# Sums of squares, token sums and weight sums in other places of a hybrid encoder block

## The chip, the cores and the metric

The kernel runs on one core of one Trainium2 chip. The core has TensorE (matmuls, results in PSUM banks), DVE (VectorE), ACT (ScalarE) and POOL (GpSimd), and DMA transfers that here are all issued from the queue of SP (SyncE). Each engine carries out its own instructions in order. The metric is the time of one execution on the device, in microseconds (us).

## The reference, cut to what matters

One layer over 2048 tokens of width 1024, all in float32. The change lies in the first steps: the input norm, the combined projection, and what each of the two head groups makes of its columns.

```python
xn = rms_norm(h, ln_mix_g[l])               # x / sqrt(mean(x*x) + EPS) * gain
proj = xn @ w_in[l]                         # 2048 x 1024 by 1024 x 2512
y_a = mlstm_group(q, k, v, o, gates, ...)   # columns of proj; q, k: conv over tokens, silu
y_b = mla_group(c_q, c_kv, k_rope, ...)     # latent queries and keys: norm, w_uq, w_ukv, rope, softmax
h = h + concatenate([y_a, y_b]) @ w_out[l]
h = h + conv_gated_mlp(rms_norm(h, ln_ffn_g[l]), ...)
h = h + sigmoid(rms_norm(h, ple_norm_g[l]) @ w_ple_gate[l]) * rms_norm(p[l] @ w_ple_proj[l], ple_post_g[l])
return rms_norm(h, final_g)
```

## The kernel before, in words

Every float32 operand of a large product is split in two parts of a shorter type, `hi` (a cast on ACT) and `lo` (a subtraction on DVE); a product takes three matmuls (`mm3`, `prod`). The instruction order on each engine is made by a planner that follows the program's order but moves an instruction ahead when its operands are ready in the planner's model; inside `manual_schedule` the named engine keeps the program's order. Buffers are named places (`w0`, `x11`, `u2`, `t7`): taking a place again waits until its last readers are done.

**Input projection** (`in_proj`). 16 tiles of 128 tokens. For each tile x is loaded turned (`load_x`), split (`split_x`) and multiplied with 464 columns of gates and latents (`nat` with `wr`, then `rest`), and with 512 value columns (`vals`). The norm's factor of a tile, `rcol`, is made by `ssq_x` and `rms_x`: ACT squares the turned tile (L236), DVE adds the eight blocks to two (L238, L239), TensorE sums over partitions with a matrix of ones (L244), DVE scales (L248) and POOL takes the power (L249). `rest` scales the latents with it, norms and rotates them into `nn`, and `turn_rest` turns `nn` by four transposes on TensorE (L290) and stores it as `rest_d`. `norm_row` turns the factors of eight tiles into a row in memory, `r_d`.

Beside the tiles a generator, `work`, is advanced by a step after each group of matmuls: first `weight_sums`, which for six pairs of weight tiles makes the sums S1 to S4 and stores them (`sp_d`), then from the ninth tile `token_sums`, which makes the seven token operands of the first block of 1024 tokens (B11, T1, T2, B21, T3, T4, B22), and last `pair_begin`, which loads and splits the first pair's operands.

**Pairs** (`pairs`). A product of two by two blocks is done with seven block products (a Winograd form), 12 matmuls each, for 6 pairs of weight tiles and 2 blocks of tokens: 12 rounds, `i` = 0 to 11. `pair_load(i)` fetches weights and their stored sums two rounds ahead, `pair_prep(i)` splits them a round ahead. The generator `sums` in `pairs` makes the second block's token operands in the rounds 1 to 4, and `load` splits them in the rounds 5 and 6. Results are added on DVE (L511), go through the convolution (`conv`) or, for the output gate, a sigmoid, and are stored (L577) as `qk_d` and `o_d`. For the output gate the store reads the buffer of the sums (places `u0` to `u2`) in place. `gates` makes the forget and input gates of all chunks in the rounds 6 to 10, one step at each `side`.

**Latent queries** (`queries`). For each of 8 groups of 256 tokens: `rope` (TensorE, then 12 small DVE instructions, L836 to L838), `weights` (first four groups: values' weights times output weights), `turn` of the rotated queries, and `latent` in two halves. PSUM results come from `gbank`, which goes round four banks. Score banks (`bank`, four others) are used only by the input projection and the scores. `attend_begin` scores the first tile of queries after the seventh group.

**mLSTM and attention** run side by side after that; in the mLSTM the heads' outputs are scaled (L1163) by factors that POOL makes (`rsq`, L145).

## Time and profile before

| | us |
|---|---|
| median of 3 runs | 2889.65 |
| lowest and highest of the 3 | 2887.4 and 2890.66 |
| the profiled execution, whole | 2890.04 |
| its span, first to last instruction | 2887.9 |
| ACT busy in the span | 1577.4 |
| DVE busy in the span | 2138.3 |

The granted clock of TensorE over the span is 0.997 of full. The profile lists instructions by source line (L545 is line 545), engine and operands (`out<-in`). A line of a helper stands for all who call it: L122 and L125 are the two halves of every split, L135 every matmul of `mm3`. Idle time before an instruction is put down to what released it ("<-DVE uv L511"). The order of time gives for each piece its start, its length from the first start to the last end, and how many instructions were merged; ends of matmuls are modelled and reach into the next one.

### The profile page before, as it was taken

How to read it: one execution, taken by the hardware profiler on the slowest of the kernel's cores; microseconds unless marked ns; L12 is line 12 of the kernel's file. 1: busy time of each engine (PE TensorE's matmuls, PEld its weight loads, DVE VectorE, ACT ScalarE, POOL GpSimd, SP SyncE). 2: the span in 40 equal slices, each digit the busy share in tenths (PEclk: the TensorE clock that was granted, in tenths of full speed). 3: DMA queues.
4: the chain of work that ended last, by engine and by line, in shares of the span. 5: the costliest groups of instructions: out<-in, count | busy, mean ns of one | idle time of the engine just before them, and what ended most of it. 6: DMA issues, size and time to landing. Idle time of an engine off the chain costs nothing.

```text
span 2887.9 us, 40258 instructions
## 1 busy us (share of the span) xinstructions
PE 2822.1 (98%) x13970; PEld 2364.1 (82%) x13970; DVE 2138.3 (74%) x3751; ACT 1577.4 (55%) x3037; POOL 213.0 (7%) x331
## 2 busy tenths in 40 slices
...
GB/s 250 239 218 285 248 186 233 173 164 145 126 136 115 97 106 111 114 239 290 276 142 167 198 167 148 221 182 237 232 229 211 239 185 252 162 267 209 280 201 164
DMA packets 455139, 566.36 MB, mean 196 GB/s; under 512 B 35316, under 2 KB 303640, under 8 KB 454936
## 3 DMA queue, kind: packets, MB, share of 16 engines
...
q8 instruction: 110, 1.80, 0.3%
q14 instruction: 93, 0.76, 0.1%
...
## 4 chain that ended last, share of the span: by engine, by line
PE 77%; DMA 8%; DVE 6%; ACT 4%; issue 3%; POOL 1%; SPq 1%; POOLq 0%; ACTq 0%; DVEq 0%
PE fy L1736 21%; PE fz L1736 14%; PE fx L1736 14%; PE ppv L1275 3%; PE tb L1263 3%; PE bk L135 2%; PE bk L1203 2%; PE bk L1200 2%; PE bk L1204 2%; PE bk L1201 2%; PE bk L1202 2%; PE ppv L1276 2%; PE fs L135 1%; PE fy L545 1%; DMA fwr<-in_w_in 1%
## 5 line engine op out<-in xcount | busy, mean ns | idle before, releaser
L1736 PE MATMUL fz<-op,fw 128*128 128x512 f32 x1968 | 478.8, 392 | 4.2 <-ACT fw L122 4.2
L1736 PE MATMUL fx<-op,fw 128*128 128x512 f32 x1968 | 476.6, 390 | 2.1 <-ACT fy L1849 1.2
L1736 PE MATMUL fy<-op,fw 128*128 128x512 f32 x1968 | 475.0, 390 | 0.0
L1736 PEld LDWEIGHTS fz<-op,fw 128*128 128x128 f32 x1968 | 368.4, 188 | 81.7 <-ACT fw L122 5.0
L1736 PEld LDWEIGHTS fx<-op,fw 128*128 128x128 f32 x1968 | 368.0, 188 | 79.2 <-ACT fy L1849 1.6
L1736 PEld LDWEIGHTS fy<-op,fw 128*128 128x128 f32 x1968 | 368.6, 188 | 76.5 <-DVE fh L1721 0.2
L122 ACT CAST pt<-tb 128x512 fp32r<-128x512 f32 x256 | 147.0, 586 | 198.9 <-PE tb L1263 198.0
L1736 PE MATMUL fy<-op,fwd 128*128 128x512 f32 (+1 forms) x984 | 238.5, 390 | 0.5 <-DVE p L1721 0.3
L1205 DVE TENSOR_REDUCE mx<-bk 128x1 f32<-128x512 f32 x256 | 174.9, 685 | 65.5 <-PE bk L1204 63.1
L1736 PEld LDWEIGHTS fy<-op,fwd 128*128 128x128 f32 x984 | 182.5, 188 | 38.9 <-DVE p L1721 0.8
L125 DVE TENSOR_TENSOR pt<-tb,pt 128x512 fp32r<-128x512 f32 x256 | 173.3, 685 | 34.4 <-ACT pt L122 33.0
L1275 PE MATMUL ppv<-pt,kv 128*128 128x512 f32 x512 | 187.9, 406 | 1.0 <-DVE pt L125 1.0
L1222 ACT ACTIVATE pe<-bk,nm 128x512 f32<-128x512 f32 x256 | 174.5, 698 | 17.8 <-DVE nm L1216 16.4
L125 DVE TENSOR_TENSOR op<-opr,op 128x512 fp32r<-128x512 f32 x205 | 134.0, 690 | 34.2 <-ACT op L122 34.2
L122 ACT CAST op<-opr 128x512 fp32r<-128x512 f32 x205 | 119.8, 620 | 71.4 <-DMA opr<-tw_d 16.5
L1263 PE MATMUL tb<-ident,pe 128*128 128x128 f32 x1024 | 150.7, 273 | 3.4 <-DVE pt L125 3.2
L1276 PE MATMUL ppv<-pt,kv 128*128 128x256 f32 x512 | 144.0, 281 | 0.0
L1263 PEld LDWEIGHTS tb<-ident,pe 128*128 128x128 f32 x1024 | 122.3, 140 | 23.6 <-DVE pt L125 6.0
L125 DVE TENSOR_TENSOR fw<-fwr,fw 128x1024 fp32r<-128x1024 f32 x100 | 122.0, 1220 | 24.3 <-ACT fw L122 24.3
L122 ACT CAST fw<-hraw 128x1024 fp32r<-128x1024 f32 (+1 forms) x72 | 70.2, 980 | 115.7 <-PE fx L1736 58.9
L1784 DVE SCALAR_TENSOR_TENSOR fgv<-uv,fcw,fgv 128x1024 f32<-128x1024 f32 x88 | 112.8, 1282 | 16.9 <-ACT fgv L1782 16.2
L122 ACT CAST fw<-fwr 128x1024 fp32r<-128x1024 f32 x100 | 105.0, 1051 | 36.4 <-DVE fwr L1710 21.6
...
## 6 DMA issues: line engine op xcount, KB each, us to landing
fwr<-in_w_up SPq DMA_DIRECT2D x66, 512.0 KB, 4.9
fh<-h_d SPq DMA_DIRECT2D x48, 512.0 KB, 4.5
h_d<-fh SPq DMA_DIRECT2D x48, 512.0 KB, 4.1
s_d<-fwr SPq DMA_DIRECT2D x44, 512.0 KB, 2.7
fws<-s_d SPq DMA_DIRECT2D x44, 512.0 KB, 4.2
rw<-row_d SPq DMA_DIRECT2D x32, 512.0 KB, 5.4
...
```

The costliest lines, as they stand in the source:

```text
L122: nc.scalar.copy(hi, src)
L125: (sub or nc.vector).tensor_tensor(lo, src, _f(hi), op=ALU.subtract)
L135: mm = lambda *a, **k: self.nc.tensor.matmul(*a, **k, skip_group_check=more)
L1200: mm(ps, ql, kh[:, ks], start=True, stop=False)
L1201: mm(ps, qr, self.krl[:, ks], start=False, stop=False)
L1205: nc.vector.tensor_reduce(s.mx[:, kb:kb + 1], ps, axis=AX.X, op=ALU.max)
L1222: nc.scalar.activation(s.pe[:, kb % 2], s.banks[kb], AF.Exp, bias=s.nm, accum_out=s.rs[:, kb:kb + 1])
L1263: nc.tensor.transpose(t[:, j, :], s.p[kb][:, j * P:(j + 1) * P], self.ident)
L1275: mm(w.ps, vh[:, ks], pts[kb][:, j], start=kt == 0, stop=False, skip_group_check=True)
L1276: mm(w.ps[:, 0], vl[:, ks], pts[kb][:, j, 0], start=False, stop=kt == NT - 1, skip_group_check=True)
L1736: nc.tensor.matmul(out, a[:, k * P:(k + 1) * P], parts[lo][:, cols], start=first, stop=lo == 1 and k == last, skip_group_check=more)
L1784: nc.vector.scalar_tensor_tensor(t, u[:, tap:tap + 2 * SB], self.taps[:, tap, ct:ct + 1], t, op0=ALU.mult, op1=ALU.add)
```

## The change

The sums of squares are taken from a second load of x, by rows: `square` loads 128 tokens by 1024 and lets one ACT instruction square and add them up; POOL scales and takes the power. All 16 are issued by the fifth tile. The factors' rows follow at the fifth and seventh tile, and `token_sums` makes both blocks' operands in the input projection, from the sixth tile on (the second block's are stored). `weight_sums` and `sp_d` are gone: `pair_load` fetches both weight tiles whole and `pair_prep` makes the four sums for each pair, in both blocks. `turn_rest` runs a tile later. At the start ACT has one small instruction ahead of the data, x is fetched ahead of the weights, and TensorE runs 26 transposes ahead of the first product. In the pairs, `gates` moves from the rounds 6 to 10 to 1 to 4, every second `side`; the output gate is stored from the places `w7` and `w11`; two edge copies move from DVE to ACT; the last round's two remaining products change places. In the latent queries the first six groups' `rope` and second half of `latent`, and all of `weights`, use score banks; the splits of keys and values are spread over groups; the first scores come a group earlier. In the mLSTM one of four pauses moves ahead of L1163.

```diff
-        self.sp_d = dt([6, 2, P, D], F32, name="sp_d")
...
-        def ssq_x(st):
-            sq = self.at("u2", [P, KT, P], name="x_sq")
-            nc.scalar.activation(sq, xq[st], AF.Square)
-            t = ss[st] = self.at("t7", [P, 4, P], name="x_ss")
-            nc.vector.tensor_tensor(t, sq[:, 0:4], sq[:, 4:8], op=ALU.add)
-            nc.vector.tensor_tensor(t[:, 0:2], t[:, 0:2], t[:, 2:4], op=ALU.add)
-
-        def rms_x(st):
-            ps = self.pml.tile([P, 4], F32, name="ssp", tag="ml")
-            for i in range(2):
-                m = nc.tensor.matmul(ps, ss[st][:, i], ones, start=i == 0, stop=i == 1)
-                if i == 0:
-                    self.tc.keep_in_program_order(m)
-            t = self.stat(1, "rsm")
-            nc.vector.tensor_scalar(t, ps[:, 0:1], 1.0 / D, EPS, op0=ALU.mult, op1=ALU.add)
-            nc.gpsimd.tensor_tensor(rcol[:, st:st + 1], t, self.nhalf[:, :1], op=ALU.pow)
-
-        def nat(st, ws, n):
+        rows = _rot("", ("u2", "x10", "x11"))
+
+        def square(st):
+            t = self.at(next(rows), [P, D], name="x_row")
+            nc.sync.dma_start(t, d["x"][0, st * P:(st + 1) * P, :])
+            sq = self.stat(1, "nt_s")
+            nc.scalar.activation(t, t, AF.Square, accum_out=sq)
+            self.rsq(sq, 1, 1.0 / D, rcol[:, st:st + 1])
+
+        def nat(st, ws, n, warm=0):
             ps = self.bank()
+            for _ in range(warm):
+                nc.tensor.transpose(ps[:, :P], self.ident, self.ident)
...
+        nc.scalar.activation(self.stat(1, "warm"), self.nhalf[:, 0:1], AF.Copy, scale=2.0)
         load_x(0)
         raws = []
         for f in range(2):
-            raws.append(load_raw(OFF_R, NREST, f, 2))
...
             nc.sync.dma_start(xq[0][:, fs], d["x_turned"][:, fs, 0:P])
             split_x(0, fs)
+            raws.append(load_raw(OFF_R, NREST, f, 2))
         raws += [load_raw(OFF_R, NREST, k2) for k2 in (2, 3)]
         wr = split_w(raws, NREST, rest_place)
         load_x(1)
+        square(0)
+        split_x(1)
...
-        ssq_x(0)
-        split_x(1)
         raws = [load_raw(OFF_V, 512, k2) for k2 in range(4)]
-        ps = nat(0, wr, NREST)
-        rms_x(0)
-        rest(0, ps)
-        ssq_x(1)
+        square(1)
+        rest(0, nat(0, wr, NREST, 26))
         wv = split_w(raws, 512, val_place)
         load_x(2)
-        ps = nat(1, wr, NREST)
-        rms_x(1)
-        rest(1, ps)
+        rest(1, nat(1, wr, NREST))
...
+        work = chain(self.token_sums(), self.pair_begin())
...
+            if st in (4, 6):
+                norm_row(st // 2 - 2)
...
+            rest(st, nat(st, wr, NREST))
+            if st < 5:
+                for q in range(4 * st - 4, 4 * st):
+                    square(q)
+            else:
+                next(work, None)
+            turn_rest(st - 1)
...
-    def weight_sums(self):
-
-        nc = self.nc
...
-            tt(v[:, hi], v[:, lo], v[:, hi], op=ALU.add)
-            tt(v[:, lo], g[:, lo], v[:, lo], op=ALU.subtract)
-            nc.sync.dma_start(self.sp_d[pr, 0], v)
-            yield
...
+            if i < 7:
+                nxt = load(i + 1)
...
+            store(blk, "B22", k, b[:, H])
+            if blk:
+                store(blk, "B11", k, a[:, L])
+                store(blk, "B21", k, b[:, L])
+                yield
+                tt(a[:, H], a[:, H], a[:, L], op=ALU.subtract)
+                store(blk, "T1", k, a[:, H])
+                c = self.at("u2", [P, 2, SB], name="xsc")
+                tt(c[:, 0], b[:, H], a[:, H], op=ALU.subtract)
+                store(blk, "T2", k, c[:, 0])
+                yield
+                tt(c[:, 1], c[:, 0], a[:, L], op=ALU.subtract)
+                store(blk, "T3", k, c[:, 1])
+                t4 = self.at("t7", [P, SB], name="xsd")
+                tt(t4, b[:, L], c[:, 0], op=ALU.subtract)
+                store(blk, "T4", k, t4)
+                yield
+                continue
...
     def pair_load(self, i):
 
-        nc, pr = self.nc, i % 6
-        g = self.at("w12", [P, KT, P], name="fwr")
-        nc.sync.dma_start(g, self.w_tile(pr, 0))
-        v = self.at("w13", [P, 4, P], name="fwr")
-        nc.sync.dma_start(v, self.w_tile(pr, 1, 4))
-        sv, sg = [self.at(t, [P, D], name="fws") for t in ("w0", "w1")]
-        nc.sync.dma_start(sv, self.sp_d[pr, 0])
-        nc.sync.dma_start(sg, self.sp_d[pr, 1])
-        self.raw[i] = g, v, sv, sg
+        raw = []
+        for e in range(2):
+            t = self.at(("w12", "w13", "w0", "w1")[i % 2 * 2 + e], [P, KT, P], name="fwr")
+            self.nc.sync.dma_start(t, self.w_tile(i % 6, e))
+            raw.append(t.rearrange("p k c -> p (k c)"))
+        self.raw[i] = raw
 
     def pair_prep(self, i):
 
-        flat = lambda t: t.rearrange("p k c -> p (k c)")
-        g, v, sv, sg = self.raw.pop(i)
+        tt = self.nc.vector.tensor_tensor
+        lo, hi = slice(0, SB), slice(SB, 2 * SB)
+        g, v = self.raw.pop(i)
         ops = self.ops[i] = {}
-        ops["A11"], ops["A12"] = self.up_pair(flat(g))
+        ops["A11"], ops["A12"] = self.up_pair(g)
+        d = self.at(("w10", "w2")[i % 2] if i else "u0", [P, 2, SB], F32R, "fwd")
+        self.split(v[:, hi], d[:, 0], d[:, 1])
+        ops["A22"] = d[:, 0], d[:, 1]
         yield
-        ops["S3"], ops["S1"] = self.up_pair(sv)
+        tt(v[:, hi], v[:, lo], v[:, hi], op=ALU.add)
+        tt(v[:, lo], g[:, lo], v[:, lo], op=ALU.subtract)
+        ops["S3"], ops["S1"] = self.up_pair(v)
         yield
-        ops["S2"], ops["S4"] = self.up_pair(sg)
+        tt(g[:, lo], v[:, hi], g[:, lo], op=ALU.subtract)
+        tt(g[:, hi], g[:, hi], g[:, lo], op=ALU.subtract)
+        ops["S2"], ops["S4"] = self.up_pair(g)
         yield
-        d = self.at(("w10", "w2")[i % 2], [P, 2, SB], F32R, "fwd")
-        self.split(flat(v), d[:, 0], d[:, 1])
-        ops["A22"] = d[:, 0], d[:, 1]
 
     def pair_begin(self):
 
         self.npair = 1
         self.pair_load(0)
+        self.pair_load(1)
         yield
         yield
-        self.begun = self.pair_prep(0)
-        for _ in range(3):
-            next(self.begun)
-            yield
+        yield from self.pair_prep(0)
...
-                t = u[:, 1:1 + 2 * SB]
-                nc.scalar.activation(t, t, AF.Copy, scale=go[:, h:h + 1])
+                t = self.at(("w7", "w11")[half], [P, 2 * SB], name="ct")
+                nc.scalar.activation(t, u[:, 1:1 + 2 * SB], AF.Copy, scale=go[:, h:h + 1])
...
-                    nc.vector.tensor_copy(edge[:, ch:ch + 1], u[:, 2 * SB:2 * SB + 1])
-                    nc.vector.tensor_copy(part[:, ch:ch + 1], t[:, 2 * SB - 1:2 * SB])
+                    nc.scalar.copy(edge[:, ch:ch + 1], u[:, 2 * SB:2 * SB + 1])
+                    nc.scalar.copy(part[:, ch:ch + 1], t[:, 2 * SB - 1:2 * SB])
...
-        def sums():
...
-                for i in (1, 3, 0, 2):
-                    nc.sync.dma_start(t[i], d["x_turned"][:, k + i // 2 * 4, (2 + i % 2) * SB:(3 + i % 2) * SB])
...
+        gates, prev = self.gates(), None
...
-                if gates:
+                if 0 < i < 5 and at % 2:
                     self.gate_bank = prev.spare if at % 2 else s.spare
                     next(gates, None)
...
+        rest_z(prev)
         rest_y(prev)
-        rest_z(prev)
...
-        w = [self.at(t, [P, D], F32R, "woa") for t in (("w7", "w11"), ("w3", "w4"))[h % 2]]
+        t = self.at(("x3", "x7")[h % 2], [P, 2, D], F32R, "woa")
+        w = t[:, 0], t[:, 1]
...
-                ps = self.gbank()
+                ps = self.bank()
...
-            ps = self.gbank([P, 2, NH, 64], "qpr")
+            ps = (self.bank if c < 6 else self.gbank)([P, 2, NH, 64], "qpr")
...
-            ps = self.gbank([P, 2, 256])
+            ps = (self.bank if half and c < 6 else self.gbank)([P, 2, 256])
...
-                if c == 1:
-                    self.vh, self.vl = self.split_latent(2, ("x10", "x11"))
-                if c == 2:
-                    self.kr2, self.krl = self.split_latent(1, ("x14", "x15"))
+                if c in (1, 3):
+                    kr = self.split_latent(1, ("x14", "x15"), (c - 1, c), None if c == 1 else kr)
+                if c in (4, 5, 6, 7):
+                    vv = self.split_latent(2, ("x10", "x11"), (c - 4,), None if c == 4 else vv)
...
+                    self.kr2, self.krl = kr
                     att = self.attend_begin()
                     next(att)
-                if c == 6:
-                    next(att)
-            next(att)
+                if c > 4:
+                    next(att, None)
...
             r4 = self.rsq(ssq, NH, 1.0 / P)
+            yield
             nc.vector.tensor_tensor(hh, hh, r4.unsqueeze(2).broadcast_to([P, NH, P]), op=ALU.mult)
-            yield from pause(4)
+            yield from pause(3)
```

129 lines of the change are left out of this document (31 added, 98 removed).

## The prediction

> **What bounds the kernel now.** I read the head of the page first, for the share of each engine, then the busy time by stage, then who waited for whom on TensorE, and last the order of time around each wait.
>
> ```profile
> span 2887.9 us, 40258 instructions
> ...
> PE 2822.1 (98%) x13970; PEld 2364.1 (82%) x13970; DVE 2138.3 (74%) x3751; ACT 1577.4 (55%) x3037; POOL 213.0 (7%) x331
> ```
>
> TensorE is busy for 2822.1 of 2887.9 us, so the whole of its idle time is 65.8 us. A change can win only a part of these, the matmuls that it removes, and the time that matmuls run below full clock. The diff touches the stages up to the end of the latent queries, and one line of the mLSTM beside attention. Those stages, cut where one follows the other (the columns: the stretch and its length; busy time and number of instructions of TensorE, its weight loads, DVE, ACT and POOL; granted clock; share of the DMA engines and their GB/s):
>
> ```profile
> 0.00:20.00 20.00, 12.38 (x50) 11.00 (x51) 11.87 (x24) 13.71 (x23) 2.14 (x10) 1.00 0.92 288
> 20.00:64.00 44.00, 42.09 (x205) 35.05 (x204) 30.61 (x81) 18.44 (x33) 8.44 (x14) 1.00 0.76 235
> 64.00:202.50 138.50, 133.68 (x648) 112.84 (x647) 95.99 (x250) 58.48 (x115) 24.51 (x47) 1.00 0.72 226
> 202.50:335.00 132.50, 124.18 (x535) 100.38 (x533) 94.01 (x143) 79.99 (x112) 0.00 (x0) 0.99 0.88 283
> 335.00:446.90 111.90, 109.58 (x495) 90.11 (x494) 74.56 (x146) 79.29 (x110) 0.00 (x0) 1.00 0.64 194
> 446.90:520.00 73.10, 59.88 (x394) 53.81 (x393) 44.03 (x137) 33.79 (x60) 0.00 (x0) 0.95 0.73 218
> ```
>
> Up to 20.00 the input projection starts, to 202.50 it runs, to 446.90 the pairs run, to 520.00 the latent queries. TensorE's busy time over the six adds up to 481.79 us, so 38.2 of the 65.8 us of idle time lie in the first 18% of the span. DVE is nowhere the bound on the mean (0.71 in the fourth row), but the DMAs are close to it there, at 0.88 and 283 GB/s. What TensorE waited for in these 520 us:
>
> ```profile
> PE bk L135 <- DVE xh L125: 7.6, 1, 7.6
> PE fy L545 <- DVE uv L511: 5.1, 3, 2.6
> PE gb L135 <- DVE qtt L837: 5.0, 3, 1.7
> PE fy L545 <- DVE uv L563: 4.1, 3, 2.8
> PE rtp L290 <- DVE nn L274: 3.6, 6, 1.5
> PE qpr L135 <- ACT woo L819: 3.2, 1, 3.2
> PE rtp L290 <- DVE nn L284: 2.7, 4, 1.6
> PE bk L1200 <- ACT pe L1222: 2.3, 1, 2.3
> PE qpr L135 <- DVE nm L1216: 1.5, 1, 1.5
> PE fz L545 <- DVE ug L511: 1.0, 1, 1.0
> PE gb L135 <- DVE ug L511: 0.8, 1, 0.8
> PE fz L545 <- DVE fw L125: 0.5, 1, 0.5
> ```
>
> The columns are the total, the number of times and the longest. The steps below take these rows one by one.
>
> **Squares from rows, step A.** The sums of squares on TensorE (L244) and the adds on DVE (L238, L239) go. What they hold of TensorE is read from the order of time:
>
> ```profile
> 7.62 7.60 PE L135 MATMUL bk<-wsr,xh 128*128 128x464 f32 x24 [7.62 <-DVE xh L125]
> 15.06 0.50 PE L244 MATMUL ssp<-ones,x_ss 128*128 128x4 f32 x4
> 15.43 5.27 PE L135 MATMUL bk<-wsr,xh 128*128 128x464 f32 x24
> ...
> 20.89 6.04 PE L135 MATMUL bk<-wsp,xh 128*128 128x512 f32 x24
> ```
>
> From the start of this group to the start of the next matmul it is 0.37 us. There are 16 tiles: 16 x 0.37 = **-5.9 us**. In its place come, for each tile, a 512 KB load of rows, one square on ACT with its read-out, and one more small instruction on POOL ahead of the same power. ACT's square exists already (L236, the next fence) and is one instruction as before. ACT is busy for 58.48 of 138.50 us and POOL for 24.51, so these are hidden; what they cost if the cover is gone stands with the rivals.
>
> **The start, step C.** The first matmul waits 7.62 us. The change moves the load of ACT's table ahead of the data, fetches x ahead of the weights, and runs 26 transposes on the idle TensorE. Of the 7.62 us the table is worth at most its own 1.28:
>
> ```profile
> 4.25 1.28 ACT L130 ACT_TABLE_LOAD   x1 [4.25 <-DMA wraw<-in_w_in]
> ...
> 10.43 2.39 ACT L130 ACTIVATE wsr<-wraw,gcol 128x464 fp32r<-128x464 f32 x4
> 13.05 1.05 ACT L122 CAST xh<-x_t 128x1024 fp32r<-128x1024 f32 x1 [0.23 <-DMA x_t<-in_x_turned]
> 14.00 1.06 ACT L236 ACTIVATE x_sq<-x_t 128x1024 f32<-128x1024 f32 x1
> ```
> ```profile
> 14.13 1.22 DVE L125 TENSOR_TENSOR xh<-x_t,xh 128x1024 fp32r<-128x1024 f32 x1
> ```
>
> The first group ran 24 matmuls in 7.60 us, the second in 5.27, so a clock that is up earlier is worth 2.3 us more. Yet neither shortens the path: the second tile's x was cast at 13.05, right when it landed (0.23 us of waiting), its lower part came out of DVE at 15.35, and the second group started at 15.43. Ahead of that load stand the same bytes as before, at 288 GB/s, and the row loads are issued behind it. So the first group ends earlier, near 13 (the cast of its last weights ended at 12.82), TensorE waits some 2.5 us, and the second group starts where it did. I take **+1.0 us**. The bounds: -2.9 if the load of x lands earlier and both gains come through (1.28 for the table, and of the 2.3 what the landing leaves, taken as 1.6), and +2.5 if the hole lets the clock fall, so that the second group too takes 7.6 instead of 5.27.
>
> That the clock falls after a hole is seen further on. 12 matmuls of 512 columns took 4.59 us after a wait of 2.65, where 24 took 6.04 at 20.89; 12 of 256 columns took 2.93 after one of 3.15, against 1.60 in the run of the work:
>
> ```profile
> 330.04 4.59 PE L545 MATMUL fy<-op,fwd 128*128 128x512 f32 x12 [2.65 <-DVE uv L511]
> ```
> ```profile
> 460.43 2.93 PE L135 MATMUL qpr<-wq,cq 128*128 128x256 f32 x12 [3.15 <-ACT woo L819]
> 463.16 2.76 PE L135 MATMUL gb<-woa,uvs 128*128 128x512 f32 x6
> ...
> 471.40 1.60 PE L135 MATMUL qpr<-wq,cq 128*128 128x256 f32 x12
> ```
>
> [...]
>
> **Turned latents a group later, step B.** The four transposes of a tile's latents (L290) now stand one tile back, so the chain ACT, POOL, DVE that makes `nn` has a whole tile's matmuls (over 11 us) instead of one group. The rows "PE rtp" go: 3.6 + 2.7 = **-6.3 us**. `nn` and `rt` change no buffers; the store of `rest_d` is only later. Nothing reads it before the last pairs.
>
> **Token sums and weights' sums, step D.** In the input projection the sums of the weights go (24 adds of 0.69 us, with 12 stores) and the second block's token sums come in. Both are DVE's, which has 42 us free in the 138.5 of the third row, and lose the x_ss adds besides. The second stage row is 44 x 235 = 10.3 MB; the 14 rows of x behind the first two add 7.3, and some 4 of the weights' sums leave (an estimate: five loads and three stores of 0.5 MB by then). Up to about 77 us, where the last square is needed, that and 13 us of tiles (1.3 MB) make 14.9 MB in 57 us, 261 GB/s, below the 288 of the first row. A load of 512 KB by full rows lands in 4.5 us elsewhere in this kernel:
>
> ```profile
> fh<-h_d SPq DMA_DIRECT2D x48, 512.0 KB, 4.5
> ```
>
> I cost this at nothing. In the pairs the price and the gain are on DVE. Each of the 11 pairs made there gains four adds:
>
> ```profile
> L407 DVE TENSOR_TENSOR fwr<-fwr 128x512 f32<-128x512 f32 x6 | 4.2, 692 | 11.0 <-DMA fwr<-in_w_in 11.0
> ```
> ```profile
> L608 DVE SCALAR_TENSOR_TENSOR tsum<-tsum,gcol,rrow 128x512 f32<-128x512 f32 x16 | 11.8, 747 | 5.9 <-DMA tsum<-in_x_turned 5.9
> ```
>
> 4 x 0.69 = 2.8 us a pair, 30 us in all. Out go the 16 scalings (11.8) and 16 subtractions (16 x 0.69 = 11.0) of the second block, 23 us, all of them in the second to fifth pair; the gates' small instructions come to those same pairs. So DVE's sum in the pairs hardly moves. What does move is what it waits for. In its own order of time it stood still for tokens just ahead of two of the late sums:
>
> ```profile
> 236.49 1.42 DVE L608 SCALAR_TENSOR_TENSOR tsum<-tsum,gcol,rrow 128x512 f32<-128x512 f32 x2 [1.65 <-DMA tsum<-in_x_turned]
> ...
> 329.29 0.69 DVE L511 TENSOR_TENSOR uv<-p,fy 128x512 f32<-128x512 f32 x1 [2.62 <-DMA o_d<-ug]
> ```
>
> The first kind ends with the token loads, and the pairs' DMAs (0.88 of the engines) lose the reloads of weight sums. The second is a buffer that the store of the o columns reads in place; that store now reads `ct`, so the buffer is free once ACT has copied it. The rows of "PE fy" and "PE fz" and the wait of "gb" for `ug` are 5.1 + 4.1 + 1.0 + 0.5 + 0.8 = 11.5 us, and the slow group at 330.04 adds 4.59 - 6.04 / 2 = 1.6: -13.1. One pair's four adds I leave exposed where DVE is tightest, the sixth pair, which also splits 20 operands (20 x 0.69 = 13.8 us of its 19): +2.8. Step D is **-10.3 us**; bounds -13.1 and +3 (all waits stay as long as they are, and the sixth pair's adds show).
>
> **Latent queries, step E.** Five or six score-sized results for each group of 256 tokens went through four banks, so the next product waited for DVE's rope (5.0 in 3) and for a copy of ACT's that itself waited for the o store's buffer (3.2). Now up to four go to the score banks, two stay, and both causes end. The score rows (2.3 and 1.5) shrink, since the first scores come one group of 256 tokens earlier and have two groups to be evaluated in, not one. The slow clock after 457.28 goes with the wait: 2.93 - 1.60 = 1.33, and in the six matmuls behind it 2.76 - 6.04 / 4 = 1.25, together 2.6. I take 5.0 + 3.2 + 2.6 and 2.2 of the 3.8: **-13.0 us**; bounds -14.6 and 0. The splits that were hoisted into the last pair are spread over later groups, under matmuls.
>
> **The mLSTM's pause, step F.** A yield ahead of L1163 moves it one step from POOL's power:
>
> ```profile
>   POOL rsr L145: 13.9, 13
> ...
>   PE mb L1167: 3.0, 3
> ```
>
> DVE stood still for 13.9 us in 13 pieces there, and TensorE behind it for 3.0. The pauses add up to what they were. I take **-2.0 us** (bounds -3.0 and 0).
>
> **The sum.** -5.9 + 1.0 - 6.3 - 10.3 - 13.0 - 2.0 = -36.5 us. The profiled execution took 2890.04 us, 2.1 more than its span; that is 0.4 above the median of 2889.65. So the forecast is 2890.04 - 36.5 = **2853.5 us**, and in the runs' terms 2853.
>
> **The rivals.** *DVE takes the place of the DMAs in the pairs.* For it: the adds sit between two products, in DVE's strict order, ahead of the sums that TensorE waits for, and the sixth pair already has 13.8 us of splits, three big subtractions of 1.22 and now 2.8 more. Against it: 0.71 busy on the mean. Then step D gives its 10.3 back and 3 more: 2867.
>
> *The banks do not help.* If the latent queries wait because DVE and ACT are late, not because banks are few, the change doesn't do what it says there, and E's 13.0 stays: 2866. Against it: at 0.60 of the last row's time DVE and ACT have room.
>
> *The rows come late: slower.* The place is the second row of norms, which is transposed on TensorE at the seventh tile and needs all 16 squares. It stands in TensorE's order at about 77 us: 15.4 + 5.1 for the second group, two groups of value columns of some 5.7, and 4 tiles of about 11.2 (5.1 + 5.7 and the four transposes). The rows are issued from about 6 us on, so TensorE stalls once a row takes more than (77 - 6) / 16 = 4.4 us. With three buffers in flight a row takes (4.5 + 1.25) / 3 = 1.9. If SP, which waits in order for a buffer behind ACT's squares, gets them through one at a time behind token loads, each takes some 5.75 plus 1.2 of waiting in ACT's line, about 7: 16 x (7 - 4.4) = 42 us of stall against 36.5 of gain: 2890.04 + 42 - 36.5 = 2895.5. It decides against the change from 4.4 + 36.5 / 16 = 6.7 us a row. Against it: ACT is busy for 0.42 of the time in the second and third rows.
>
> **How the numbers follow.** Forecast 0.60, with a range of its own of 2846 to 2862; DVE 0.17; the banks 0.13; rows late 0.08; no change, by several part costs at once, 0.02. The range runs from 2842, near the sum of all lower bounds (-5.9 - 2.9 - 6.3 - 13.1 - 14.6 - 3.0 = -45.8, 2844), to 2877, which takes in both rivals on the fast side and the second group's fall of the clock. It leaves out the slow rival and tails of 0.07, some 0.15. The measurement can tell about 0.2%, 5.8 us, from no change: faster 0.90, within 0.02, slower 0.08.
>
> **What would show it.** A: no L244, no gap ahead of the third tile's products. B: no wait of L290. C: the first matmul near 6 us, the second group still near 15.4. D: no wait of TensorE for `uv` above 1 us before the sixth pair. E: the stretch from the last pair's end to 520 us shorter by some 13 us, no wait for `qtt`. F: no idle time of DVE ahead of the line that is L1163 now. Wrong: a busy TensorE above 2820 us, a new wait at the transposes of the norms, or DVE above 0.9 in the fifth to seventh pair with TensorE behind it.

## The result and the profile after

The changed kernel took 2875.88 us (median of 4 runs, 2871.88 to 2876.72), the kernel before 2890.15 us beside it (4 runs, 2887.4 to 2892.21). The ratio is 0.9948, with a 95% interval of 0.9931 to 0.9966: faster by 14 us, where 36.5 had been forecast. The profiled execution of the changed kernel took 2876.04 us. Its head, and its stages cut where they follow each other as before (up to 20.00 the start, to 204.85 the input projection, to 443.60 the pairs with the first six matmuls on the output weights, to 514.70 the latent queries; the columns are those of the table of before):

```profile
span 2874.3 us, 40054 instructions
...
PE 2818.0 (98%) x13932; PEld 2357.9 (82%) x13932; DVE 2133.7 (74%) x3702; ACT 1581.6 (55%) x3071; POOL 211.0 (7%) x347
```
```profile
0.00:20.00 20.00, 16.09 (x72) 12.38 (x73) 10.73 (x20) 13.49 (x22) 1.43 (x8) 1.00 0.91 309
20.00:64.00 44.00, 43.85 (x207) 36.63 (x206) 18.56 (x58) 24.55 (x54) 14.18 (x34) 1.00 0.81 250
64.00:204.85 140.85, 128.41 (x586) 106.23 (x585) 100.70 (x233) 53.58 (x116) 18.42 (x44) 0.98 0.84 267
204.85:335.00 130.15, 127.68 (x565) 104.11 (x564) 99.51 (x180) 92.33 (x142) 0.00 (x0) 1.00 0.55 160
335.00:443.60 108.60, 108.00 (x482) 88.83 (x482) 76.62 (x110) 75.74 (x101) 0.00 (x0) 1.00 0.55 165
443.60:514.70 71.10, 63.72 (x439) 57.93 (x438) 48.17 (x146) 36.66 (x72) 0.00 (x0) 0.95 0.83 250
```

The reader is to look at TensorE's busy time against the length. In the second row only 0.15 us are idle, in the fourth and fifth 3.1 of 238.75. But the third row has 12.4 idle, far from the 4.8 of its counterpart before, and its granted clock fell to 0.98. The sixth has 7.4. Whom TensorE waited for up to 514.70 (total, times, longest):

```profile
PE rtp L281 <- DVE nn L265: 6.7, 4, 5.2
PE bk L1142 <- DVE q_s L124: 4.7, 1, 4.7
PE rtp L281 <- DVE nn L275: 4.2, 7, 1.3
PE bk L134 <- DVE xh L124: 2.9, 2, 1.5
...
```

The turns of the latents (L281, which was L290) still wait, now 10.9 us instead of 6.3, and the second row is new. By stage, with the span of both profiled executions as the sum:

| stage | before, us | after, us | difference | forecast |
|---|---|---|---|---|
| to the pairs' first matmul (A, B, C) | 202.52 | 204.85 | +2.3 | -11.2 |
| pairs, to the first rotary matmul (D) | 250.3 | 238.75 | -11.5 | -10.3 |
| latent queries, to the first product with the values (E) | 77.8 | 71.1 | -6.7 | -13.0 |
| first to last product with the values (F) | 698.5 | 699.5 | +1.0 | -2.0 |
| the rest, not edited | 1658.8 | 1660.1 | +1.3 | 0 |
| span | 2887.9 | 2874.3 | -13.6 | -36.5 |

So D came as forecast; 13.5 us are missing in the first row, 6.3 in the third and 3.0 in the fourth. In the input projection the first stretch did go as planned: the fifth tile's products start at 54.63 instead of 58.97. What was won there is lost afterwards, above all at the end:

```profile
83.12 0.59 PE L281 MATMUL rtp<-ident,nn 128*128 128x128 f32 x3 [0.68 <-DVE nn L265]
```
```profile
190.30 0.90 PE L281 MATMUL rtp<-ident,nn 128*128 128x128 f32 x3 [5.16 <-DVE nn L265]
...
191.50 13.15 PE L134 MATMUL bk<-wsp,xh 128*128 128x512 f32 x48
204.50 0.60 PE L281 MATMUL rtp<-ident,nn 128*128 128x128 f32 x4
204.85 0.48 PE L606 MATMUL fy<-op,fw 128*128 128x512 f32 x1
```

The wait of 5.16 us stands at the turn of tile 14 (tiles are numbered from 0 here, so the fifth is tile 4), and the 48 matmuls behind it take 13.0 us up to 204.50, where two groups in the run of the work take 11.1. The turns of the middle tiles, from 83 to 133, wait for 4.35 us. DVE makes `nn`, and its busy time in the first four stretches of 12 us there (shown are the first stretch and the sum of all) was before:

```profile
83.00:95.00 12.00, 7.59 (x21) 1.00 0.93 299
...
sum 48.00, DVE 30.11; mean DVE 7.53
```

And after:

```profile
83.00:95.00 12.00, 10.80 (x25) 1.00 0.80 230
...
sum 48.00, DVE 43.58; mean DVE 10.89
```

From 0.63 of the time it went to 0.91, though over the whole third stage it is at 0.71 (0.69 before). Its load alone does not make the waits, however. The kernel before had nearly the same load later, with the first block's token sums there:

```profile
119.00:131.00 12.00, 10.29 (x25) 1.00 0.47 156
...
sum 48.00, DVE 42.71; mean DVE 10.68
```

That is 0.89 of the time, and the turns waited only 1.2 us in these 48 us.

The new wait in the latent queries, on TensorE and on SP:

```profile
481.44 0.80 PE L1142 MATMUL bk<-kv,q_s 128*128 128x512 f32 x1 [4.66 <-DVE q_s L124]
...
485.45 0.59 PE L1146 MATMUL bk<-kv,q_s 128*128 128x512 f32 x1
485.88 0.40 PE L1142 MATMUL bk<-kv,q_s 128*128 128x512 f32 x1
```
```profile
472.88 3.07 SPq L805 DMA_DIRECT2D q_d<-qso  x4
476.00 0.59 SPq L792 DMA_DIRECT2D q_d<-qo  x1
476.69 1.58 SPq L1124 DMA_DIRECT2D q_t<-q_d  x2
```

The first scores are ready to run at 476.8, but their queries' loads left SP only at 476.69, behind five stores. The ten matmuls after the hole start 0.43 us apart, the later ones 0.23: 2 us more. The granted clock was 0.50 from 481.00 to 485.50 and 1.00 from 485.90 to 487.00.

### The profile page after: what moved, and what is told of

The parts are those of the page before. It is cut to its first block, busy times and chain, and to the rows that moved or that the text cites. A ratio compares the mean times of both kernels' runs of the same rounds, so it can differ in the third digit from the quotient of the medians.

```text
span 2874.3 us, 40054 instructions
## 1 busy us (share of the span) xinstructions
PE 2818.0 (98%) x13932; PEld 2357.9 (82%) x13932; DVE 2133.7 (74%) x3702; ACT 1581.6 (55%) x3071; POOL 211.0 (7%) x347
## 4 chain that ended last, share of the span: by engine, by line
PE 79%; DMA 4%; DVE 3%; ACT 3%; issue 2%; POOL 0%; SPq 0%; POOLq 0%; ACTq 0%; DVEq 0%
PE fy L1678 21%; PE fz L1678 14%; PE fx L1678 14%; PE ppv L1217 3%; PE tb L1205 3%; PE bk L1142 2%; PE bk L1146 2%; PE bk L1144 2%; PE bk L1145 2%; PE bk L1143 2%; PE fy L525 2%; PE ppv L1218 2%; PE fs L134 2%; PE fx L525 1%; PE mb L1081 1%
## 5 line engine op out<-in xcount | busy, mean ns | idle before, releaser
L1678 PE MATMUL fx<-op,fw 128*128 128x512 f32 x1968 | 476.8, 390 | 3.2 <-ACT fy L1791 1.7
L1678 PE MATMUL fy<-op,fwd 128*128 128x512 f32 (+1 forms) x984 | 238.6, 390 | 0.4 <-DVE uv L1663 0.4
L124 DVE TENSOR_TENSOR fw<-fwr,fw 128x1024 fp32r<-128x1024 f32 x124 | 150.7, 1220 | 35.9 <-ACT fw L121 35.8
L121 ACT CAST fw<-fwr 128x1024 fp32r<-128x1024 f32 x124 | 129.4, 1050 | 48.6 <-DVE fwr L1652 23.0
L1218 PE MATMUL ppv<-pt,kv 128*128 128x256 f32 x512 | 144.1, 281 | 0.0
```

Of the source, the lines that this page charges most:

```text
L121: nc.scalar.copy(hi, src)
L124: (sub or nc.vector).tensor_tensor(lo, src, _f(hi), op=ALU.subtract)
L1218: mm(w.ps[:, 0], vl[:, ks], pts[kb][:, j, 0], start=False, stop=kt == NT - 1, skip_group_check=True)
L1678: nc.tensor.matmul(out, a[:, k * P:(k + 1) * P], parts[lo][:, cols], start=first, stop=lo == 1 and k == last, skip_group_check=more)
```

## The experiments

All of them start from the changed kernel. The table gives four stretches of each run's profile and its median with the ratio to the kernel before, run beside it: *tiles* from the taps' transpose ahead of the fifth tile's products to the pairs' first matmul, *pairs* and *latent* as in the table above, *mLSTM* from the first to the last product with the values.

| kernel | tiles | pairs | latent | mLSTM | median, us | ratio (95%) |
|---|---|---|---|---|---|---|
| before | 143.7 | 250.3 | 77.8 | 698.5 | 2890.15 | 1 |
| before, once more | 143.3 | 255.1 | 76.1 | 699.0 | 2895.5 | one run |
| changed | 150.4 | 238.8 | 71.1 | 699.5 | 2875.88 | 0.9948 (0.9931 to 0.9966) |
| queries a block earlier | 151.1 | 238.3 | 67.5 | 699.1 | 2874.07 | 0.9946 (0.993 to 0.9963) |
| first sums' load a tile earlier | 150.6 | 237.4 | 72.0 | 700.6 | 2874.18 | 0.9945 (0.993 to 0.9959) |
| sums of i = 6 in x10 | 150.0 | 237.2 | 70.4 | 699.3 | 2875.06 | 0.9944 (0.9929 to 0.9959) |
| two places for xsc | 152.9 | 238.7 | 71.1 | 699.5 | 2879.93 | 0.996 (0.9945 to 0.9975) |
| tile 14's turn behind its values | 145.1 | 243.7 | 70.8 | 699.5 | 2875.57 | 0.9952 (0.9937 to 0.9966) |
| sums mixed, row in tile 5 | 156.3 | 237.4 | 70.5 | 698.6 | 2878.59 | 0.9962 (0.9945 to 0.9978) |
| sums mixed, row in tile 6 | 151.7 | 237.1 | 70.5 | 699.5 | 2876.56 | 0.9948 (0.9933 to 0.9963) |
| rest's copy first | 144.1 | 240.7 | 71.4 | 699.4 | 2872.48 | 0.9944 (0.9929 to 0.9959) |
| queries two blocks earlier, u2 | 152.6 | 238.3 | 63.8 | 699.1 | 2869.19 | 0.9932 (0.9917 to 0.9947) |
| turn without lag | 144.2 | 240.5 | 71.6 | 699.1 | 2878.54 | 0.9962 (0.995 to 0.9973) |
| pause put back | 152.1 | 238.6 | 70.9 | 700.0 | 2877.82 | 0.9962 (0.995 to 0.9974) |
| copy first, queries early | 143.9 | 240.1 | 63.7 | 700.5 | 2866.32 | 0.9916 (0.9901 to 0.993) |
| five edits | 145.7 | 238.8 | 64.3 | 701.4 | 2865.56 | 0.9909 (0.9893 to 0.9926) |
| load early in place of x10 | 141.1 | 243.5 | 63.7 | 699.7 | 2866.86 | 0.9918 (0.9905 to 0.9931) |
| and operands apart | 142.0 | 243.6 | 64.0 | 701.9 | 2867.4 | 0.9916 (0.9902 to 0.9931) |

Where an edit does not touch a stretch, the stretch still moves between profiles: by 2.2 us in *tiles* (150.4 to 152.6 in the rows whose edit lies elsewhere), by 3.3 in *mLSTM*, and by 4.8 in *pairs* between the two profiles of the kernel before. Effects of a few us are therefore read from the wait that they remove, not from the median alone.

### The loads of the first scores' queries

```diff
-                if c == 4:
+                if c == 3:
                     self.kr2, self.krl = kr
                     att = self.attend_begin()
-                    next(att)
-                if c > 4:
+                if c > 2:
                     next(att, None)
```

`attend_begin` has one more `yield` between its loads and its split.

> Changed kernel, with the loads of the first scores' queries issued one block of latent queries earlier (block 3 instead of 4) and the split and the scores left where they were. Theory (TensorE's 4.66 us wait for q_s at 481.44 is a late load: SP takes it up behind four stores of turned queries): the wait falls under 1.5 us, the 10 matmuls after it run at 0.23 instead of 0.43 us, 441.5 to the first joint score is 4 to 6 us shorter than the 64.1 of the changed kernel, the time is near 2871. Rival (place w2, which the split of block 5 shares, or VectorE sets it): the wait stays above 3 us and the time at 2876.

The wait fell from 4.66 to 1.76 us, between the 1.5 of the theory and the 3 of the rival, and *latent* by 3.6. So the late issue was most of it. What is left has two bounds close together: the second of the two loads, issued at 471.28, landed 6.0 us later, at 477.2, and the split's place w2 holds block 5's operands until 476.8. Which of the two counts more was not taken apart; the next edit takes both away, with loads behind block 2 and the place u2:

```diff
-            qs = self.at("u2" if (h, pr) != (0, 0) else "w2", [P, 2, 256], F32R, "q_s")
+            qs = self.at("u2", [P, 2, 256], F32R, "q_s")
```

> Changed kernel, with the first scores' queries loaded two blocks earlier (behind block 2) and split into u2 instead of w2. Theory (with the load one block earlier 1.76 us of the wait were left, since the split's place w2 is that of block 5's operands, whose last matmul ends only at the scores' turn): the wait goes below 0.3 us, the first scores' matmuls stay at 0.23 us each, the first multiplication by the values comes 6 to 7.5 us earlier than in the changed kernel, counted from the end of the pairs. Rival (the split stands behind other work on ScalarE or VectorE): 1 us or more of the wait stays.

*Latent* is 63.8, 7.3 shorter than in the changed kernel, and no wait for q_s is left. What TensorE still waits for in the stretch (444 to 510):

```profile
PE bk L1142 <- ACT pe L1164: 1.4, 1, 1.4
PE gb L800 <- DVE v L968: 1.2, 1, 1.2
```

The theory holds.

### The first sums' load, and two places

```diff
                 for q in range(4 * st - 4, 4 * st):
                     square(q)
+                if st == 4:
+                    next(work, None)
```

> Changed kernel, with the first step of the token sums (which issues the first two loads) taken in tile 4 instead of tile 5. Theory (VectorE stands 5.74 us at 79.36 before the first sum's load, is then nearly full and never catches up, so that the normalized rows of tiles 5 to 14 come late to TensorE's turns): that wait falls to 0 to 2 us, TensorE's waits of L281 on VectorE (10.9 us in total before 204.85) fall under 6, the first pair's first matmul is at 196 to 201 instead of 204.85, the time near 2870. Rival (the chain of each tile itself, gates on VectorE, rest on ScalarE, its squares, the power on GpSimd, two products, is longer than a tile's 11.4 us of matmuls): the waits of L281 stay at 9 us or more, the first matmul stays at 203 to 206, the time at 2876.

In the changed kernel DVE had stood 5.74 us before the first scaling of a sum:

```profile
79.36 1.28 DVE L415 SCALAR_TENSOR_TENSOR xsr<-xsr,gcol,rrow 128x1024 f32<-128x1024 f32 x1 [5.74 <-DMA xsr<-in_x_turned]
```

With the earlier load this became 3.2 us for the row of factors and 1.0 for the tokens, yet L281 waited 10.8 us (10.9 before the edit) and *tiles* stayed at 150.6. The theory of the late load falls, taken alone.

```diff
+            ab = self.at("x10", [P, 2, 2 * SB], name="xsr2") if i == 6 else None
             for e in range(2):
-                t = self.at(("w12", "w13", "w0", "w1")[i % 2 * 2 + e], [P, 2 * SB], name="xsr")
+                t = ab[:, e] if i == 6 else self.at(("w12", "w13", "w0", "w1")[i % 2 * 2 + e], [P, 2 * SB], name="xsr")
```

> Changed kernel, with the two loads of the token sums of i = 6 put into place x10 instead of w12 and w13, so that the first pair's weights can be loaded there while those sums are still stored. Theory (the end of the stage, 5.16 us at 190.30 and the 13.15 us of cold matmuls behind it, comes of the pair's loads being late at 179.35, ScalarE's cast standing on them ahead of the last tiles' rests): ScalarE's 6.88 us at 183.65 and TensorE's 5.16 us go, the first pair's first matmul is at 196 to 200, the time near 2870. Rival (VectorE is late there by its own load): the pair's loads are earlier but TensorE still stands 4 us or more on the normalized rows of the last two tiles, first matmul at 203 or later, the time at 2876.

The place was not what held the pair's loads. They left SP at 179.40 (179.35 in the changed kernel), right behind the last store of the sums, and ACT stood for them as long as before. In the changed kernel, ahead of tile 14's copy:

```profile
183.65 1.05 ACT L121 CAST fw<-fwr 128x1024 fp32r<-128x1024 f32 x1 [6.88 <-DMA fwr<-in_w_in]
...
186.63 0.63 ACT L255 ACTIVATE rs<-bk,rcol 128x448 f32<-128x448 f32 x1
```

And with the edit:

```profile
183.78 1.04 ACT L121 CAST fw<-fwr 128x1024 fp32r<-128x1024 f32 x1 [6.96 <-DMA fwr<-in_w_in]
```

TensorE's 5.16 us became 2.00 only because the group ahead of the turn came later: tile 15's split of x made TensorE wait 3.52 instead of 1.35, with 24 matmuls in 6.81 us behind it. The turn stood at 190.88 (190.30 before the edit), and the pairs began at 204.31. So this run says nothing for or against the theory that ACT's stand for the pair's weights makes the turn late, and no run took that stand alone away.

```diff
-                c = self.at("u2", [P, 2, SB], name="xsc")
+                c = self.at(("u2", "w3")[i % 2], [P, 2, SB], name="xsc")
```

> Changed kernel, with the two difference tiles of the second block's token sums in two places by turns (u2 and w3) instead of u2 alone. Theory (VectorE's waits for the stores of these tiles, 5.3 us in three, keep it late in tiles 10 to 14): the waits of xsc on xo_d go, TensorE's waits of L281 between 150 and 204.85 fall from 6.5 us to under 3, first matmul at 200 to 202, the time 2872. Rival (VectorE's work there, not the stores, keeps it late, the wait moves to the next sum's loads): xsr waits instead, first matmul within 1 us of 204.85, the time at 2876.

A miss: DVE's waits of 5.3 us for these stores turned into 7.0 us at the third difference tile (`xsd`), whose place is single as well. The rival had named another load; the wait moved within DVE's own stores, and *tiles* did not shrink.

### The order at the last tiles

```diff
+            if st == NT - 1:
+                vals(st - 1)
             turn_rest(st - 1)
             if st == NT - 2:
                 continue
-            if st == NT - 1:
-                vals(st - 1)
```

> Changed kernel, with one line moved: in the last tile the values of tile 14 are multiplied ahead of the turn of tile 14's normalized rows, not behind it. Theory (the change hands the turn of a tile one tile of time, but tile 14 has no value matmuls of its own, so that its turn comes only one group, 5.2 us, behind its rest, and the chain takes some 12 us): the 5.16 us wait at 190.30 and the slow clock behind it (48 matmuls in 13.0 us where two groups take 11.4) both go, the turn of tile 14 waits under 0.5 us, that of tile 15 up to 1 us, the first pair's first matmul is at 197.5 to 199.5 instead of 204.85, the time near 2869. Rival (the rows come late there whatever stands between, from the pair's operands queued ahead of them): the wait moves to tile 15's turn at 4 us or more, first matmul at 202 or later, the time near 2875.

The wait at the turn went, as the theory said: 0.48 us where there were 5.16, and the pairs begin at 199.39. But the pairs gave 4.9 us back:

```profile
192.04 0.33 PE L281 MATMUL rtp<-ident,nn 128*128 128x128 f32 x1 [0.48 <-DVE nn L275]
...
199.39 0.50 PE L606 MATMUL fy<-op,fw 128*128 128x512 f32 x1 [0.33 <-DVE vo L289]
...
208.67 5.49 PE L525 MATMUL fy<-op,fw 128*128 128x512 f32 x12 [3.31 <-ACT fy L608]
```
```profile
202.29 0.62 ACT L121 CAST op<-opr 128x512 fp32r<-128x512 f32 x1 [4.00 <-DMA opr<-xo_d]
...
208.04 0.58 ACT L608 COPY fy<-fx 128x512 f32<-128x512 f32 x1
```

TensorE waits for a copy of ACT's that stands behind casts of the next token operands, and ACT stands 4.00 us for their load. Behind the wait the twelve matmuls took 5.49 us, against 2.9 ahead of it. So the end of the projection hid a second bound that lies only 5 us behind.

### The chain of a tile, and what DVE has to do

```diff
+            rs = self.at(f"t{st % 2}", [P, 448], name="rs")
+            nc.scalar.activation(rs, ps[:, 16:NREST], AF.Copy, scale=rx)
             for i, o in ((0, st), (8, NT - 1 - st)):
                 nc.vector.scalar_tensor_tensor(self.gt[:, i:i + 8, o], ps[:, i:i + 8], rx, bg[:, i:i + 8],
                                                op0=ALU.mult, op1=ALU.add)
-            rs = self.at(f"t{st % 2}", [P, 448], name="rs")
-            nc.scalar.activation(rs, ps[:, 16:NREST], AF.Copy, scale=rx)
```

> Changed kernel, with ScalarE's copy of the rest placed ahead of VectorE's two gate products, so that the products follow the copy and not the copy the products. Theory (the chain of a tile passes twice through VectorE, which is full: the gate products, on which the copy waits, 28.6 us in eight, and the normalization): one of the two passages goes, the normalized rows are ready 3 us or more sooner, TensorE's waits of L281 before 185 fall from 5.6 us to under 2, that at 190.30 from 5.16 to 3 or less, first matmul at 198 to 201. Rival (VectorE's amount of work in these tiles is the bound, and the chain only follows it): waits and first matmul as before within 1 us.

*Tiles* fell to 144.1 and the pairs began at 197.88; their end came 5.0 us earlier than in the changed kernel. In the changed kernel ACT's copy stood 28.6 us, in eight tiles, for the gate products on DVE, although it reads nothing of theirs. From tile 9 on no turn waits, tile after tile in 10.95 us (the turns at 141.41 and 152.35), but tile 14's does, 4.28 us of the former 5.16, and its copy stands behind a cast of ACT's that waited 9.39 us for the first pair's weights:

```profile
184.76 1.11 PE L281 MATMUL rtp<-ident,nn 128*128 128x128 f32 x4 [4.28 <-DVE nn L265]
```

The waits before 185, tile 14's left out, fell from 5.6 to 4.2 us only, against the 2 expected: the tiles 5 to 8 still take some 12 us each, and the turn of tile 9 is no nearer to the taps' transpose (76.7 us) than it was (76.8). The theory holds for the later tiles, the rival for the tiles 5 to 8. In those the copy is asked for first and still starts late. Tile 8's products end at 106.6, and its copy starts at 114.06, behind ACT's casts of the first block's sums, which wait for DVE:

```profile
112.33 0.62 ACT L121 CAST op<-xsr 128x512 fp32r<-128x512 f32 x1 [2.03 <-DVE xsr L439]
...
114.06 0.63 ACT L252 ACTIVATE rs<-bk,rcol 128x448 f32<-128x448 f32 x1
```

So the chain still goes through DVE twice there, now by way of ACT's order. A copy ahead of these casts was not tried.

Next, the sums in another order, to make the work of these four tiles less:

```diff
-            if st in (4, 6):
-                norm_row(st // 2 - 2)
+            if st in (4, 5):
+                norm_row(st - 4)
...
+        order = ((0, 0), (0, 1), (1, 0), (0, 2), (1, 1), (0, 3), (1, 2), (1, 3))
         def load(i):
-            blk, k = divmod(i, 4)
+            blk, k = order[i]
```

> Changed kernel, with the token sums of both blocks taken by turns (first, first, second, first, second, first, second, second) instead of four of the first and then four of the second, and the second block's row of reciprocals made one tile earlier. Theory (in tiles 5 to 8 VectorE has 12 us of work of its own per tile, two scalings of 1.28, four sums and four halves of splits of 0.69, the next tile's split of 1.23 and some 3 us of the rest, against 11.3 us of TensorE's, and is the bound there): the mean work is 11 us, the periods of the tiles 6 to 9 fall from 11.9 to 12.4 towards 11.4, TensorE's waits of L281 between 83 and 133 fall from 4.35 us to under 2, first matmul 2 to 3 us earlier. Rival (the chain of one tile sets it, whatever else VectorE does): these waits stay at 3.5 us or more.

The row a tile earlier came too early: TensorE's transpose of the second row of norms stood 8.12 us for the factors. Behind that hole the tiles go at full pace:

```profile
73.83 0.37 PE L294 MATMUL tb<-ident,rcol 128*8 128x128 f32 x1 [8.12 <-POOL rcol L144]
...
92.64 0.60 PE L281 MATMUL rtp<-ident,nn 128*128 128x128 f32 x4
...
103.59 0.60 PE L281 MATMUL rtp<-ident,nn 128*128 128x128 f32 x4
```

10.95 us a tile with no wait, where the changed kernel takes 12. That could be the mixing or the 8 us that DVE was given. So the mixing was run without the hole:

> Changed kernel, with the token sums of both blocks by turns as in the run with the mixed sums, but the second block's row of reciprocals made in tile 6, as in the changed kernel. Theory (VectorE's amount of work in tiles 5 to 8 is the bound): no wait of 8 us at the row, periods of tiles 6 to 9 near 11.0 to 11.5 us, TensorE's waits of L281 between 83 and 133 under 2 us in total instead of 4.35, from the first matmul of tile 4 (54.63 in the changed kernel) to the pairs 145 to 148 us instead of 150.2. Rival (the chain): these waits stay at 3.5 us or more and the stretch at 150.

The waits between 83 and 133 were 3.8 us instead of 4.35 and *tiles* 151.7: the rival, by its own numbers. Less work alone does not help; why the tiles ran at full pace behind the hole is not shown.

The lag of the turns was undone, too (for the last two tiles also as before the change):

```diff
-            turn_rest(st - 1)
...
             vals(st)
+            turn_rest(st)
```

> Changed kernel, with the turn of a tile's normalized rows back behind the same tile's values, as before the change, all else changed. Theory (the chain of a tile has grown from some 6 to some 12 us by VectorE's added work in tiles 5 to 14, so that the lag of a tile, on which the prediction counted for 6.3 us, is eaten by it but still needed): without it TensorE waits some 5 to 6 us in each of the tiles 5 to 8 and 1 to 4 in the later ones, L281's waits are 30 us or more in total instead of 10.9, first matmul of the pairs at 220 or later, time 2890 or more. Rival (the chain has its length only because the later turn lets VectorE's other work go first, and would be as short as before if asked for earlier): L281's waits 6 to 12 us, first matmul at 198 to 206, time 2870 to 2877.

The rival, clearly: L281 waited 8.5 us in all between 60 and 204, not 30, and the pairs began at 203.08, 1.8 us earlier than with the lag.

```profile
PE rtp L281 <- DVE nn L275: 4.8, 6, 1.3
PE rtp L281 <- DVE nn L265: 3.1, 2, 2.0
```

Ahead of the sums the lag does work. Without it, tile 2's turn waits, the 24 matmuls behind it take 6.85 us instead of 5.2, and the taps' transpose is at 58.89, against 54.42:

```profile
45.77 0.70 PE L281 MATMUL rtp<-ident,nn 128*128 128x128 f32 x4 [2.17 <-DVE nn L265]
46.23 6.85 PE L134 MATMUL bk<-wsr,xh 128*128 128x464 f32 x24
```

So the lag is worth 4.5 us to the fifth tile and costs 6.2 from there on (144.2 against 150.4), most of it at tile 14, whose order alone made 5.3 (145.1 above).

### The mLSTM's pause

```diff
-            yield
             nc.vector.tensor_tensor(hh, hh, r4.unsqueeze(2).broadcast_to([P, NH, P]), op=ALU.mult)
-            yield from pause(3)
+            yield from pause(4)
```

> Changed kernel, with the mLSTM's last scaling of hh put back where it stood before the change: right behind the reciprocal root, and four pauses behind it instead of one ahead and three behind. Theory (the step that the change put ahead of the scaling leaves the four transposes one step less behind the scaling, so that TensorE waits for hy and its neighbours 4.0 us in four instead of 3.0 in three): first to last multiplication by the values falls from 699.4 us (699.1 to 700.6 in the runs of the changed kernel and of its variants so far) to 698.5, as before the change, and the time by 1 us. Prediction's step F (the later scaling saves 2 us): 701 or more. Rival (the wait comes of something else that was moved there): 699.4 still, waits for hy 3.8 to 4.1 us.

The stretch *mLSTM* took 700.0 us, and the waits for `hy` 3.8 us in three, against 4.0 in four with the change. The waits are as the rival had them, and the stretch is 0.6 off its 699.4. The kernel before was profiled again:

> The kernel before, unchanged, profiled once more. If the step of the mLSTM made a difference, first to last multiplication by the values is again 698.5 us, plus or minus 0.3, and 1659 us follow it. If the difference is what one profile has against another, this stretch is between 698 and 701 and the rest between 1657 and 1663.

699.0 this time, and 1660.8 us behind it; the changed kernel and its variants lie between 698.6 and 701.9. The difference of +1.0 is not above what one profile has against another. That the pause does anything, good or bad, was not shown.

### Several edits together

> Changed kernel, with two of the single edits together: the rest's copy ahead of the gate products, and the first scores' queries loaded two blocks earlier and split into u2. If the two losses are separate (one in the input projection, one in the latent queries) the gains add: 5.0 us to the end of the pairs and 7.1 behind it, first multiplication by the values at 502 to 504, time 2862 to 2867. Rival (the second only takes up what the first leaves): 507 or later, time 2869.

The gains add: *tiles* 143.9 and *latent* 63.7, each as alone; 2866.32 us. This kernel beats the changed one with two small edits.

> Changed kernel, with five single edits together: both blocks' sums by turns (second block's row made in tile 6 as in the changed kernel), the rest's copy ahead of the gate products, tile 14's turn behind its values, the sums of i = 6 in x10, the queries two blocks earlier. Theory (three causes in the input projection, VectorE's amount of work in tiles 5 to 8, its double passage in each tile's chain, the order at the end, each with a wait of its own): TensorE's waits of L281 fall from 10.9 to under 3 us, the pairs' first matmul to 189 to 194; the first pair then waits 2 to 5 us for operands whose places the last tiles' rests hold, first multiplication by the values at 495 to 501, time 2857 to 2864. Rival (the operands of the first pair set that point whatever the projection does, as after the turn alone, 0.7 us of 5.5 kept): the pairs end no earlier than with the copy first alone (436.5), time as with two edits.

The turn of tile 14 no longer waits, but new waits came at the turns of the tiles 4 and 5 (1.23, 1.10 and 1.07 us, and 24 matmuls in 7.30 us) and at tile 15's split (2.18). *Tiles* is 145.7, the pairs begin at 199.70 instead of the 189 to 194 expected. No better than two edits.

> As the kernel with five edits, but with the first sums' loads a tile earlier (step of the token sums in tile 4) in place of the sums of i = 6 in x10. Theory (with VectorE's amount of work spread, its stand before the first sum's load, which cost nothing while that amount was the bound, is now what TensorE meets at 71.8 and 84.3, 3.4 us and 1.6 us of slow clock; and x10 for i = 6 is what makes tile 15's split late, 2.18 us at 181.25): from the first matmul of tile 4 to the pairs 138 to 141 us instead of 145.5, the first multiplication by the values 1 to 5 us earlier than there counted from the same point (448.6), since the first pair's operands come no earlier, time 2857 to 2864. Rival (these waits are of the chain): 145 us, time 2866.

*Tiles* is 141.1, the shortest of all, as expected, and the waits of L281 are down to 3.6 us:

```profile
PE fy L529 <- ACT fy L612: 3.4, 1, 3.4
PE rtp L281 <- DVE nn L275: 2.1, 2, 1.6
PE rtp L281 <- DVE nn L265: 1.5, 2, 1.4
```

The early load, worth nothing alone, is worth 4.6 us here against the kernel with five edits, together with the taking back of x10; what the mixing adds was not taken apart. But the first row of the fence is the pairs' second bound again, *pairs* is 243.5, and the median stays. The last run asked for that bound: the first four token operands of the pairs in two places of their own, w3 and w4.

```diff
+        o2 = [self.at(p, [P, 2, SB], name="opr2") for p in ("w3", "w4")]
+        first = [t[:, e] for t in o2 for e in range(2)]
...
-                raw = self.at(next(rot), [P, SB], name="opr")
+                if first:
+                    raw = first.pop(0)
+                else:
+                    raw = self.at(next(rot), [P, SB], name="opr")
```

> As the last kernel (sums by turns and loaded a tile earlier, rest's copy first, tile 14's turn behind its values, queries early), with the first four of the first pair's token operands loaded into w3 and w4 instead of the places of the last two tiles' rests. Theory (SP issues these loads only when the rests of tiles 14 and 15 have left t0 to t3, at 194.8 to 200 us, ScalarE stands 5.04 us on them at 198.66, and TensorE 3.43 us on the copy queued behind them, with a slow group after): ScalarE's stand falls under 2 us, TensorE's 3.43 us under 1, from the pairs' first matmul to that of the latent queries' rotary part 238.5 to 240.5 us instead of 243.5, time 3 to 5 us less than there. Rival (the pair's weights or the order on SP set it): the stretch stays at 242 or more.

The rival: *pairs* 243.6, ACT's stand 4.57 us. The places are free, but SP is not:

```profile
186.06 0.39 SPq L511 DMA_DIRECT2D opr<-xo_d  x1
190.28 2.29 SPq L458 DMA_DIRECT2D fwr<-in_w_in  x2
194.13 0.34 SPq L267 DMA_DIRECT2D vv_d<-nn  x1
194.56 0.38 SPq L511 DMA_DIRECT2D opr<-xo_d  x1
```

Between the first and the second operand SP takes the second pair's two weight tiles and the store of the last tile's `nn`. The second operand leaves right behind that store. That moving them would bring the pairs forward was not tried.

## Why the prediction was right or wrong

**The sum** was 36.5 us and 13.6 came in the profile. The sign, the range of 2842 to 2877 and the chance of faster held; the likeliest one's own range of 2846 to 2862 did not. That the time lies within the wide range is luck: its upper end stood for the rivals in the pairs and at the banks and for a fall of the clock at the start, none of which came, and what was lost in the input projection is in no term of it. Step B failed, E left a wait out, and F did not do what it was for.

**A, right.** No sum of squares on TensorE is left, and each group of 464 columns is followed by the next matmul without the 0.37 us. No wait of TensorE's names ACT's squares or POOL's powers. The rival of the late rows was wrong, but it was closer than its 0.08 says: in the changed kernel the sixteenth norm was there at 72.6, 4.5 us ahead of its transpose at 77.13, and asked for a tile earlier it was waited for, for 8.12 us. On the mean that is (72.6 - 6) / 16 = 4.2 us a row, not 1.9, against the 4.4 from which TensorE would have stalled. It is the pace at which the rows were asked for, four to a tile and the last four from 59.71 on, and not what one row takes.

**C, right in kind.** The first matmul started at 5.72 instead of 7.62, and the second group at 15.43, exactly as before; the hole ahead of it was 1.53 us and the group took 5.31. The step cost 0 instead of +1.0, which was the author's estimate between the two bounds, and the clock did not fall there (granted 1.00 from 15.43 to 20.74). Behind the 26 transposes the 24 matmuls of the first group took 376 ns each in the median, before the change 542. That the clock is the cause was not shown: it is granted at 1.00 both times, from 7.60 to 15.40 before and from 5.70 to 15.43 after.

**B, the step that failed.** The chain that makes `nn` "has a whole tile's matmuls (over 11 us) instead of one group", so the rows "PE rtp" were to go. They grew from 6.3 to 10.9 us. With the 1.9 us that the 48 matmuls behind the longest wait took too much, and the 1.35 at tile 15's split of x, less the 1.0 that C did not cost, that is nearly all of the 13.5 us missing up to the pairs. Two things in the step were wrong.

First, the lag does not reach tile 14: in the last two tiles its values are held back, and only one group, from 179.85 to some 185, lies between its rest and its turn. That was to be read in the diff. Moving the line took the 5.16 us away, and the slow matmuls behind it, though the pairs then gave 4.9 us back.

Second, the chain did not keep its length, but grew with the lag: in the tiles 6 to 14 ACT's copy started 0.5 to 3.3 us behind the end of its products before the change, and 7.3 to 8.6 us behind it after. Two of the chain's links are DVE's, and step D put the token sums into the same engine in the same tiles. With the sums left there and tile 14's order as before the turns waited 8.5 us without the lag and 7.1 with it: of the tile handed over, 1.4 us came of it.

The prediction took DVE's free time as a mean, "42 us free in the 138.5", where four tiles went from 0.63 to 0.91 busy. The mean held (0.71, and 0.69 before) and said nothing on those tiles. Nor does the 0.91 by itself: at 0.89, without a lag, the turns before waited 1.2 us. A nearer theory, that DVE's late start or its amount of work alone was the cause, fell as well: either edit alone left *tiles* at 150.6 and 151.7. What counted alone, beside the order at tile 14, was the copy behind the gate products, which sent each tile's chain through DVE's line twice (144.1); this won its 6.3 us from the turn of tile 9 on. What makes the tiles 5 to 8 wait stays open: ACT's order, seen there in the trace, was not put to the test. With the copy first, the load early, the sums mixed and the turn moved, *tiles* was 141.1.

**D, right where it was costed.** The pairs took 11.5 us less (10.3 forecast), though the two profiles of the kernel before differ by 4.8 there. Of the waits for `uv` one of 0.5 us is left, and DVE at 99.51 of 130.15 us did not take the DMAs' place, as the first rival had it. "I cost this at nothing", of the sums in the input projection, is the part of D that came back under B.

**E, right in mechanism, with a wait left out.** The waits for `qtt` and `woo` are gone. The prediction said that the first scores come one group earlier and counted 2.2 us for it, but not that the queries' loads then stand behind five stores on SP, or that the split's place is that of block 5's operands: 4.66 us, and 2 us of slow clock (granted 0.50). With these taken away *latent* is 63.8, 14.0 shorter than before, close to the forecast of 13.0. The rival "the banks do not help" does not fit, since the waits that it would keep are gone; no run took the banks back alone.

**F** was forecast at -2.0; with the pause, without it and before, the stretch is the same within what profiles differ by. The step counted on DVE no longer standing for POOL's power, 13.9 us in 13 pieces before. With the change it stands as long:

```profile
DVE hy L1105 <- POOL rsr L144: 14.3, 13, 1.9
```

So TensorE's waits for `hy` could not shrink by it, and did not (3.0 us before, 4.0 after, 3.8 undone). Why the stand stayed was not asked.

**What is still missing.** The shortest profile of all, with the load early in place of x10, has a span of 2863.9 us: 24.0 of the 36.5. Against the kernel before it won 7.1 us up to the pairs (11.2 forecast), 6.8 in the pairs (10.3) and 14.1 in the latent queries (13.0), and lost 1.2 and 2.8 in the last two rows. Of the 12.5 us still missing, 4.1 lie ahead of the pairs, 3.5 in them and 6.0 in the last two rows, less 1.1 of the latent queries. In the pairs the second bound is left; in the last two rows some 3 us may be what one profile has against another.
